# Splitting the output weights during the input projection and keeping both parts in DRAM

## The chip, the cores and the metric

The kernel runs on one core of a Trainium2 chip. The core has five instruction streams that matter here: TensorE (PE in the profile, with its weight loads shown apart as PEld), VectorE (DVE), ScalarE (ACT), GpSimd (POOL) and SyncE (SP), which in this kernel issues every data transfer (DMA). The metric is the device time of one execution in microseconds (us). The kernel before was timed in three runs: 2034.74, 2035.24 and 2037.11 us, median 2035.24 us. One further execution was taken under the hardware profiler; its own time was 2037.63 us and its span, from the first to the last instruction, 2035.9 us.

## The reference

One layer of a streaming encoder is computed for a prompt of 2048 frames and for 64 further frames ("sample") of a running stream with 4096 past frames. `D_MODEL` is 1024, and there are four heads of differential attention (branch A) and four of retention (branch B). Cut to what matters here:

```python
def layer_inputs(x, ...):
    h = rmsnorm(x, norm_g) @ w_in                     # 1024 -> 6144 columns
    qa, ka, va, za, qb, kb, vb, zb, ga, gb = jnp.split(h, ...)
    ...
    ga = jax.nn.sigmoid(ga + b_gate[0]); gb = jax.nn.sigmoid(gb + b_gate[1])

def layer_output(x, oa, ob, za, zb, ga, gb, ..., w_oa, w_ob, w_out):
    oa = (rmsnorm(oa, subln_g) * (1.0 - lam_init)).reshape(B, T, W_A) * jax.nn.silu(za)
    ob = rmsnorm(ob).reshape(B, T, W_B) * jax.nn.silu(zb)
    m = ga * (oa @ w_oa) + gb * (ob @ w_ob)           # w_oa, w_ob: 512 x 1024
    return x + m @ w_out                              # w_out: 1024 x 1024
```

Between the two stand the attention of branch A (prompt frames see their own and earlier chunks, the sample sees the past cache and itself) and the chunked recurrence of branch B. `w_oa` is the input `w_o_diff`, and `w_ob` is `w_o_ret`.

## The kernel before, in words

**Precision.** All large products run on operands in the fp32r format. To keep the accuracy, an operand x is split into a high part, `h` (x cast to fp32r on ScalarE), and a low part, `l` = x - h (a subtraction on GpSimd or VectorE). A product takes three matmuls: h·h, h·l and l·h. So each weight that TensorE uses has to be loaded, cast and subtracted first.

**Stages and streams.** Two streams run side by side. `w_stream` is the input projection: frames in two halves of 1024 (the first half carries the 64 sample frames too), and in each half 24 column tiles of 256 columns of `w_in`. `z_stream` is the attention and the retention: the four prompt heads of the first half, then in the first half the sample's attention (`sample_attn`), the sample's retention and retention blocks 0 to 7 (`ret_sample`, `ret_some`), then the same for the second half. When both are through, the output stage (`out_stream`) takes eight groups g of 256 frames (264 columns with the sample's): eight `m_tile`s per group (the products with `w_o_diff` and `w_o_ret`, 24 matmuls of 264 columns each), whose results `m_fin` multiplies by the gates and splits, and two `y_tile`s per group (the product with `w_out`, 48 matmuls of 512 columns each), plus one for the sample at the end.

**What sets the order.** The program is written out by a planner in Python (`loop`). Tasks are generators that yield the time or condition at which they can go on; the planner keeps a running estimate of each engine's time and always advances the ready task with the lowest priority number. `w_stream` has number 9 and `z_stream` 4, with helpers at 0 to 3, so that projection matmuls fill whatever TensorE time the other stream leaves. `out_stream` has 8. The orders on TensorE, ScalarE and VectorE are those in which the planner emits; SP and GpSimd are ordered by the tile framework. `take` and `give` count the buffers of a tag. `ld` and `st` put a DMA on SP.

**The weight pipeline of the projection.** `w_load` (lines 332 to 342) loads units of 256 rows by 256 columns (256 KB) into a staging tag `ws` of 3 buffers, in the order of `self.order`. `w_split` (line 344) takes two of the 12 buffers of tag `w`, one for the high and one for the low part, casts on ScalarE (line 354) and subtracts on GpSimd (line 361; twice, at the start, on VectorE), and appends the pair to the queue `wq`. A column tile (`natural` or `transposed`, whose matmuls are on line 384) takes four units and gives their `w` buffers back one by one during its last group of matmuls. 12 buffers are six units, so while a column tile is worked on, two units are split ahead, and three more are staged.

**The order of the first half.** `seq` in `w_stream` has, after the attention's columns, the tiles of vb, qb, kb (two each), a mark, za and zb (two each), ga and gb (four each).

**The output weights.** When `z_stream` is through, its buffers are closed, pool `z3` is opened and `load_wo` (line 1244) fetches `w_o_diff` and `w_o_ret`, in 32 pieces of 128 rows by 256 columns (128 KB). Each goes into one of the 9 buffers of tag `oz`, is cast on ScalarE (line 1232), and subtracted on GpSimd (line 1235, a third of them) or VectorE (line 1239). `out_prep` starts when the eighth pair of tiles is begun; its loads of attention output and z (three `oz` buffers per tile) feed `og_fin`, which makes the split operands of `m_tile`. When the projection is through, its pools are closed and pool `z4` is opened; there `gate_prep` loads the gates into the 6 buffers of tag `gt`, two for each `m_tile`, and `load_wout` fetches `w_out` in another 32 pieces, through the same `gt` buffers. `m_fin` gives two `gt` buffers back when it is through (line 1379). `m_tile` has two PSUM buffers for each branch, so that it runs at most two tiles ahead of `m_fin`.

Of the kernel before, what the change touches and what calls it, by code (L numbers as in the profile page):

```python
# [8 lines left out]
F32 = mybir.dt.float32  # L9
# [45 lines left out]
class Hybrid:  # L55
# [276 lines left out]
    def w_load(self):  # L332
        for half in range(2):
            for c0 in self.order[half]:
                for q in range(4):
                    yield from self.take("ws")
                    st = self.sb(self.wp, [128, 2, 256], "ws")
                    t = self.ld(st, self.i["w_in"][0, 256 * q:256 * q + 256, c0:c0 + 256]
                                .rearrange("(c p) n -> p c n", p=128), 1 << 18)
                    self.wst.append((st, t))  # L340
                    self.wloads += 1
                    yield self.pe

    def w_split(self):
        nc = self.nc
        for n in range(4 * (len(self.order[0]) + len(self.order[1]))):
# [873 lines left out]
    def split_load(self, stp, tag, h, l, src, n, slot):  # L1220
        for q in range(4):
            sl = slice(256 * q, 256 * q + 256)
            yield from self.take(tag)
            s = self.sb(stp, [128, GW], tag, "wst")[:, :256]
            t = self.ld(s, src[:, sl], 1 << 17)
            self.spawn(self.split_fin(tag, h[:, sl], l[:, sl], s, t, (n + q) % 3 == 0, slot), 2)
            yield self.pe

    def split_fin(self, tag, h, l, s, t, on_pool, slot):
        nc = self.nc  # L1230
        yield t
        nc.scalar.copy(h, s)
        t = self.A(256, self.pe)
        if on_pool:
            nc.gpsimd.tensor_sub(l, s, h.bitcast(F32))  # L1235
            t = self.G(256, t)
        else:
            yield t
            nc.vector.tensor_sub(l, s, h.bitcast(F32))
            t = self.V(256, t)  # L1240
        self.give(tag, t)
        slot.append(t)

    def load_wo(self):
        pool = self.z3
        for br, name in enumerate(("w_o_diff", "w_o_ret")):
            for kt in range(4):
                h = pool.tile([128, 1024], F32R, tag=f"{name}h{kt}", name=f"{name}h{kt}")
                l = pool.tile([128, 1024], F32R, tag=f"{name}l{kt}", name=f"{name}l{kt}")
                slot = []  # L1250
                self.wo[br].append((h, l, slot))
                yield from self.split_load(pool, "oz", h, l, self.i[name][0, 128 * kt:128 * kt + 128, :], kt, slot)

    def load_wout(self):
        pool = self.z4
        for ct in range(8):
            h = pool.tile([128, 1024], F32R, tag=f"woh{ct}", name=f"woh{ct}")
            l = pool.tile([128, 1024], F32R, tag=f"wol{ct}", name=f"wol{ct}")
            slot = []
            self.wout.append((h, l, slot))  # L1260
            yield from self.split_load(pool, "gt", h, l, self.i["w_out"][0, 128 * ct:128 * ct + 128, :], ct, slot)
# [62 lines left out]
    def m_tile(self, g, ct, og):  # L1324
# [3 lines left out]
        for br, tag in ((0, "mm"), (1, "s")):  # L1328
            yield from self.take(tag)
            ps = self.psum(tag)[:, :GW]  # L1330
            for kt in range(4):
                wh, wl, tw = self.wo[br][kt]
                if ct == 0:
                    yield lambda: len(self.ogs) > 8 * g + 4 * br + kt and self.ogs[8 * g + 4 * br + kt] and len(tw) == 4
                    og.append(self.ogs[8 * g + 4 * br + kt][0])
                    if max(*tw, og[-1][2]) > self.pe:
                        yield max(*tw, og[-1][2])
# [44 lines left out]
    def y_tile(self, g, sel, r, x, y):  # L1382
# [10 lines left out]
        for ct, nh in [(c, k) for k in range(2) for c in range(7)] + [(7, 0), (7, 1)]:  # L1393
            nsl, xt, tx, ps = run[nh]
            yield lambda: len(self.wout) > ct and len(self.wout[ct][2]) == 4 and len(self.mq[g]) > ct
# [6 lines left out]
            if max(t, *tw) > self.pe:  # L1402
                yield max(t, *tw)
# [38 lines left out]
    def w_stream(self):  # L1442
# [23 lines left out]
        seqs = [f + seq for f in first]  # L1466
        self.order = [[c for c, _ in q if c is not None] for q in seqs]
# [162 lines left out]
```

## Time and profile before

| quantity | value |
|---|---|
| median of three runs | 2035.24 us (2034.74 to 2037.11) |
| the profiled execution's own time | 2037.63 us |
| its span | 2035.9 us |
| PE busy | 1999.1 us, 98% |
| DVE busy | 985.9 us, 48% |
| ACT busy | 962.7 us, 47% |
| POOL busy | 420.5 us, 21% |
| moved by DMA | 281.57 MB, 138 GB/s in the mean |

The page gives each engine's busy time, then the span in 40 slices, the DMA queues, the chain of work that ended last, the costliest groups of instructions, and the DMA issues. Groups are rows of "line, engine, operation, output<-inputs, shapes, count | busy us, mean ns of one | idle time before them and what ended it". Durations of matmuls overlap, because they are pipelined: the time that one costs is the distance from its start to the next start. The view by windows gives busy time by engine in a stretch, with the granted clock of TensorE, the busy share of the 16 DMA engines and what they moved; for the instructions of one line it gives that line's share. Times in the timeline and in the chain are from the start of the span.

### The profile page before, as it was taken

Reading aid. Unit: us, or ns where it says so; the run is one execution under the profiler, and the core shown is the slowest. Engines: PE = TensorE matmul, PEld = TensorE weight load, DVE = VectorE, ACT = ScalarE, POOL = GpSimd, SP = SyncE. Lnnn points to the kernel's source line nnn. Section 1 sums busy time; section 2 is a strip of 40 time slices with the busy share of each in tenths; the row PEclk is TensorE's granted clock in tenths of the full one; section 3 lists DMA queues with packets and bytes.
Section 4 is the critical chain, followed back from the end, with each engine's and each line's share of the span. In section 5 each row is a group of like instructions: output and inputs, shape, how many; then the busy total and the mean of one; then the engine's idle time right before and its main releaser. Section 6 shows DMA issues by size and latency. Waiting matters only on the chain. (4 is left out here: it accounts for less than half of the span.)

```text
span 2035.9 us, 35819 instructions
## 1 busy us (share of the span) xinstructions
PE 1999.1 (98%) x13058; PEld 1826.1 (90%) x13058; DVE 985.9 (48%) x2671; ACT 962.7 (47%) x2123; POOL 420.5 (21%) x394
## 2 busy tenths in 40 slices
PE   7999999999999999999999999999999979999999
PEld 7999999999998999999999888888888868888997
DVE  6265765643331210546856545635653365444442
ACT  5334766644343332535766655634654453333321
POOL 1222112121012221221211212122131343222210
PEclk9999999999999999999999999999999989999999
DMA  6663545345565463563352252463233665454531
GB/s 217 202 195 115 162 138 145 101 124 156 151 170 133 130 194 93 152 200 127 113 155 91 84 154 75 115 188 99 63 100 113 187 200 154 144 150 136 148 101 58
DMA packets 332160, 281.57 MB, mean 138 GB/s; under 512 B 65104, under 2 KB 307408, under 8 KB 331984
## 3 DMA queue, kind: packets, MB, share of 16 engines
q1 hardware_dynamic: 331984, 279.29, 46.8%
q8 instruction: 103, 1.69, 0.4%
q14 instruction: 73, 0.60, 0.1%
HBM read 187.71 MB, written 91.49 MB: 137 GB/s over the span
## 5 line engine op out<-in xcount | busy, mean ns | idle before, releaser
L384 PE MATMUL mm<-xh,wh 128*128 128x512 f32 (+2 forms) x1280 | 459.8, 359 | 0.0
L384 PE MATMUL mm<-xh,wl 128*128 128x512 f32 (+2 forms) x1280 | 452.0, 353 | 0.0
L384 PE MATMUL mm<-xl,wh 128*128 128x512 f32 (+2 forms) x1280 | 451.7, 353 | 0.0
L361 POOL TENSOR_TENSOR wl<-ws,wh 128x512 fp32r<-128x512 f32 x190 | 252.1, 1342 | 832.5 <-ACT wh L354 643.5
L384 PE MATMUL mm<-wh,xh 128*128 128x256 f32 x1088 | 313.3, 288 | 0.5 <-ACT xh L315 0.3
L384 PE MATMUL mm<-wl,xh 128*128 128x256 f32 x1088 | 307.7, 283 | 0.7 <-DVE wl L358 0.3
L384 PE MATMUL mm<-wh,xl 128*128 128x256 f32 x1088 | 307.7, 283 | 0.2 <-DVE xl L316 0.2
L384 PEld LDWEIGHTS mm<-xh,wl 128*128 128x128 f32 x1280 | 241.0, 188 | 31.1
L384 PEld LDWEIGHTS mm<-xh,wh 128*128 128x128 f32 x1280 | 241.3, 189 | 30.6 <-issue 0.2
L384 PEld LDWEIGHTS mm<-xl,wh 128*128 128x128 f32 x1280 | 241.4, 189 | 30.0
L384 PEld LDWEIGHTS mm<-wh,xh 128*128 128x128 f32 x1088 | 204.8, 188 | 3.3 <-ACT xh L315 0.5
L384 PEld LDWEIGHTS mm<-wl,xh 128*128 128x128 f32 x1088 | 204.9, 188 | 3.0 <-DVE wl L358 0.5
L384 PEld LDWEIGHTS mm<-wh,xl 128*128 128x128 f32 x1088 | 204.7, 188 | 0.4 <-DVE xl L316 0.4
L569 ACT COPY ev<-mm 128x512 f32<-128x512 f32 x140 | 71.6, 512 | 213.4 <-PE mm L384 200.4
L865 DVE TENSOR_TENSOR atl<-at,ath 128x512 fp32r<-128x512 f32 (+1 forms) x144 | 93.6, 660 | 151.6 <-ACT ath L863 151.6
L782 ACT ACTIVATE row<-row,a_mx 128x1024 f32<-128x1024 f32 (+7 forms) x160 | 153.5, 963 | 24.2 <-DVE a_mx L762 24.0
L752 DVE CUSTOM_DVE_ANT_0 row<-s,dfar 128x512 f32<-128x512 f32 (+2 forms) x192 | 117.3, 631 | 72.4 <-PE s L744 71.3
L354 ACT CAST wh<-ws 128x512 fp32r<-128x512 f32 x192 | 117.0, 619 | 65.4 <-PE mm L384 37.5
L863 ACT CAST ath<-at 128x512 fp32r<-128x512 f32 (+1 forms) x144 | 79.6, 563 | 99.1 <-PE at L850 98.6
L743 PE MATMUL s<-K,q 128*128 128x512 f32 (+3 forms) x320 | 120.3, 381 | 3.0 <-DVE a_acc L752 2.8
L803 DVE SCALAR_TENSOR_TENSOR row<-row,a_w 128x1024 f32<-128x1024 f32 (+4 forms) x96 | 101.4, 1064 | 40.5 <-ACT row L800 40.2
L744 PE MATMUL s<-K,q 128*128 128x512 f32 (+3 forms) x320 | 115.7, 363 | 0.0
(196 smaller groups left out, 3922.1 us busy)
## 6 DMA issues: line engine op xcount, KB each, us to landing
ws<-in_w_in_dram SPq DMA_DIRECT2D x192, 256.0 KB, 3.0
q<-qT SPq DMA_DIRECT2D x128, 128.0 KB, 3.0
V<-vN SPq DMA_DIRECT2D x24, 512.0 KB, 5.4
K<-kT SPq DMA_DIRECT2D x48, 256.0 KB, 4.2
gt<-gaT SPq DMA_DIRECT2D x64, 132.0 KB, 2.1
gt<-gbT SPq DMA_DIRECT2D x64, 132.0 KB, 2.1
xt<-in_x_prompt_dram SPq DMA_DIRECT2D x16, 512.0 KB, 5.0
kn<-in_cache_k_T_dram SPq DMA_DIRECT2D x32, 256.0 KB, 3.2
```

The source lines that it names most:

```text
L354: nc.scalar.copy(h, st)
L361: nc.gpsimd.tensor_sub(l, st, h.bitcast(F32))
L384: nc.tensor.matmul(ps, p, q, start=c == 0 and i == 0, stop=c == KC - 1 and i == 2)
L569: nc.scalar.copy(ev, ps)
L743: nc.tensor.matmul(ps, q1s, kk, start=True, stop=False)
L744: nc.tensor.matmul(ps, q2s, kk, start=False, stop=True)
L752: nc.vector.tensor_tensor_reduce(out=units[k0 // 1024][:, k0 % 1024:k0 % 1024 + n], in0=ps, in1=tab, scale=-SLOPES[h], scalar=3.0e38, op0= ...
L782: nc.scalar.activation(u, u, AF.Exp, bias=mx, scale=-1.0, accum_out=lp[:, k:k + 1])
L803: nc.vector.scalar_tensor_tensor(out=u0, in0=u0, scalar=w[:, 0:1], in1=u1, op0=ALU.mult, op1=ALU.add)
L863: nc.scalar.copy(ah[:, :w], at[:, :w])
L865: nc.vector.tensor_sub(al[:, :w], at[:, :w], ah[:, :w].bitcast(F32))
```

## The change

Scratch tensors `wsp` are added in DRAM: a high and a low part for each of `w_o_diff`, `w_o_ret` (512 x 1024) and `w_out` (1024 x 1024), 16 MB together. In the first half's sequence, after each of the first six tiles of the row za0, za1, zb0, zb1, ga0, ga1, two new items stand. The eight items of the two smaller weights hold two units each (a column block of 256 over 512 rows), the four items of `w_out` hold four. So four units follow za0, za1, zb0 and zb1 each, and eight units follow ga0 and ga1 each: 32 units. They go through `w_load` and `w_split` in their place in the order; then, instead of matmuls, `presplit` takes them from `wq` and stores both parts to DRAM, and the two `w` buffers come free when the second store has landed.

In the output stage the 64 pieces with their casts and subtractions (`split_load`, `split_fin`) are gone. `load_pair` loads 128 rows by 1024 columns of each part (512 KB) straight into the tile that TensorE reads: 16 loads for the two smaller weights and 16 for `w_out`. After issuing a pair it waits until the planner's estimate for that DMA has passed. `oz` and `gt` buffers are no longer taken for weights.

```diff
+        self.wsp = {n: [tc.dram_tile([k, 1024], F32, name=f"{n}{j}") for j in range(2)]
+                    for n, k in (("w_o_diff", 512), ("w_o_ret", 512), ("w_out", 1024))}
...
     def w_load(self):
+        for name, c0, nq in self.order:
+            for q in range(nq):
+                yield from self.take("ws")
+                st = self.sb(self.wp, [128, 2, 256], "ws")
+                t = self.ld(st, self.i[name][0, 256 * q:256 * q + 256, c0:c0 + 256]
+                            .rearrange("(c p) n -> p c n", p=128), 1 << 18)
...
-    def split_load(self, stp, tag, h, l, src, n, slot):
-    def split_fin(self, tag, h, l, s, t, on_pool, slot):
+    def presplit(self, name, c0, nq):
+        for q in range(nq):
+            yield lambda: len(self.wq) > 0
+            h, l, t = self.wq.pop(0)
+            if t > self.pe:
+                yield t
+            for j, w in enumerate((h, l)):
+                ts = self.st(self.wsp[name][j][256 * q:256 * q + 256, c0:c0 + 256]
+                             .rearrange("(c p) n -> p c n", p=128), w.bitcast(F32), 1 << 18)
+            self.give("w", ts, 2)
             yield self.pe
...
+    def load_pair(self, pool, name, kt, tag, out):
+        rows = slice(128 * kt, 128 * kt + 128)
+        w = []
+        for j in range(2):
+            u = pool.tile([128, 1024], F32R, tag=f"{tag}{j}{kt}", name=f"{tag}{j}{kt}")
+            t = self.ld(u.bitcast(F32), self.wsp[name][j][rows, :], 1 << 19)
+            w.append(u)
+        out.append((w[0], w[1], t))
+        yield t - DMA_LAT
...
     def load_wo(self):
+                yield from self.load_pair(self.z3, name, kt, name, self.wo[br])
     def load_wout(self):
+            yield from self.load_pair(self.z4, "w_out", ct, "wo", self.wout)
...
+        out = [("w_o_diff", c, 2) for c in range(0, 1024, 256)] + \
+              [("w_o_ret", c, 2) for c in range(0, 1024, 256)] + [("w_out", c, 4) for c in range(0, 1024, 256)]
+        late = len(seq) - 12
+        mid = seq[:late]
+        for k, item in enumerate(seq[late:]):
+            mid.append(item)
+            if k < 6:
+                mid += [(o, None) for o in out[2 * k:2 * k + 2]]
+        seqs = [first[0] + mid, first[1] + seq]
...
+                elif f is None:
+                    yield from self.presplit(*c0)
```

In `m_tile` and `y_tile` the waits for four pieces per weight tile become one wait for the pair's load.

More of the change, by code (lines that the diff above doesn't have):

```diff
@@ L332, in w_load @@
     def w_load(self):
[L333 to L342, printed above, removed]
+        for name, c0, nq in self.order:
[4 more added lines that the diff above has]
+                            .rearrange("(c p) n -> p c n", p=128), 1 << 18)
+                self.wst.append((st, t))
+                self.wloads += 1
+                yield self.pe
     def w_split(self):
         nc = self.nc
-        for n in range(4 * (len(self.order[0]) + len(self.order[1]))):
+        for n in range(sum(o[2] for o in self.order)):
             yield lambda: len(self.wst) > 0
@@ L1218, in ret_sample @@
         self.state, self.t_state = None, 0.0
-    def split_load(self, stp, tag, h, l, src, n, slot):
[L1221 to L1226, printed above, removed]
-            yield self.pe
-    def split_fin(self, tag, h, l, s, t, on_pool, slot):
[L1230 to L1242, printed above, removed]
+    def presplit(self, name, c0, nq):
[8 more added lines that the diff above has]
+            self.give("w", ts, 2)
+            yield self.pe
@@ L1256, in load_wout @@
         for ct in range(8):
[L1257 to L1261, printed above, removed]
+            yield from self.load_pair(self.z4, "w_out", ct, "wo", self.wout)
     def out_prep(self):
@@ L1333, in m_tile @@
                 if ct == 0:
-                    yield lambda: len(self.ogs) > 8 * g + 4 * br + kt and self.ogs[8 * g + 4 * br + kt] and len(tw) == 4
+                    yield lambda: len(self.ogs) > 8 * g + 4 * br + kt and self.ogs[8 * g + 4 * br + kt]
                     og.append(self.ogs[8 * g + 4 * br + kt][0])
-                    if max(*tw, og[-1][2]) > self.pe:
-                        yield max(*tw, og[-1][2])
+                    if max(tw, og[-1][2]) > self.pe:
+                        yield max(tw, og[-1][2])
                 oh, ol, _ = og[4 * br + kt]
@@ L1394, in y_tile @@
             nsl, xt, tx, ps = run[nh]
-            yield lambda: len(self.wout) > ct and len(self.wout[ct][2]) == 4 and len(self.mq[g]) > ct
+            yield lambda: len(self.wout) > ct and len(self.mq[g]) > ct
             h, l, t = self.mq[g][ct]
@@ L1465, in w_stream @@
                             self.transposed(half, dst, 2 * g, final=fin)))
-        seqs = [f + seq for f in first]
-        self.order = [[c for c, _ in q if c is not None] for q in seqs]
+        out = [("w_o_diff", c, 2) for c in range(0, 1024, 256)] + \
[7 more added lines that the diff above has]
+        seqs = [first[0] + mid, first[1] + seq]
+        self.order = [c if isinstance(c, tuple) else ("w_in", c, 4) for q in seqs for c, _ in q if c is not None]
         self.seg_free = [0.0, 0.0]
```

11 lines of the change are left out of this document (2 added, 9 removed).

## The prediction

> **What bounds the kernel now.** I read the page first: which engine is busy, and where in the 40 slices it is not.
>
> ```profile
> span 2035.9 us, 35819 instructions
> PE 1999.1 (98%) x13058; PEld 1826.1 (90%) x13058; DVE 985.9 (48%) x2671; ACT 962.7 (47%) x2123; POOL 420.5 (21%) x394
> PE   7999999999999999999999999999999979999999
> ```
>
> TensorE is busy all the time, except in the first slice and in slice 33, where the output stage begins. So a change that leaves the matmuls as they are can gain only what that slice lacks, and any stretch in which it makes TensorE wait is lost in full. Then the waits of TensorE, the timeline around slice 33 and the chain that ended last:
>
> ```profile
> PE mm L1339 <- DVE gt L1359: 7.4, 4, 2.9
> PE s L1339 <- ACT ogh L1298: 4.6, 2, 4.3
> PE at L1404 <- ACT mh L1369: 2.0, 1, 2.0
> ```
> ```profile
> 1634.12 0.40 PE L384 MATMUL mm<-xh,wl 128*128 128x512 f32 x1
> 1634.36 0.28 PE L1339 MATMUL mm<-ogh,w_o_diffh 128*128 128x264 f32 x1
> 1634.48 0.28 PE L1340 MATMUL mm<-ogl,w_o_diffh 128*128 128x264 f32 x1
> 1642.71 0.59 PE L1339 MATMUL s<-ogh,w_o_reth 128*128 128x264 f32 x1 [4.30 <-ACT ogh L1298]
> 1643.78 0.42 PE L1339 MATMUL mm<-ogh,w_o_diffh 128*128 128x264 f32 x1
> 1644.00 0.42 PE L1340 MATMUL mm<-ogl,w_o_diffh 128*128 128x264 f32 x1
> ```
> ```profile
> 1688.95 0.70 DVE oyt L1418
> 1734.56 0.70 DVE oyt L1418
> ```
>
> The projection's last matmul starts at 1634.12, the first `m_tile` at 1634.36, and the first finished output tile is added at 1688.95: 54.6 us. Starts are 0.12 us apart for 264 columns when the clock is full (1634.36, 1634.48). One whole group takes 1734.56 - 1688.95 = 45.6 us, with 192 matmuls of 264 columns and 96 of 512; 192 x 0.122 = 23.4, so one of 512 takes (45.6 - 23.4) / 96 = 0.23 us. Up to the first finished output tile there are 192 of the one kind and 45 of the other, 33.8 us. So the beginning of the output stage costs 20.8 us too much: about 6.5 before 1643.78 (the second `m_tile`), 14.3 behind it. That is the whole of what can be won.
>
> **What goes in the output stage.** Splitting goes, 64 pieces; the groups of `w_out`, with two of the queue's rows, show the main part:
>
> ```profile
> L1232 ACT CAST woh<-wst 128x256 fp32r<-128x256 f32 x32 | 12.2, 402 | 3.8 <-DMA wst<-in_w_out_dram 3.5
> L1239 DVE TENSOR_TENSOR wol<-wst,woh 128x256 fp32r<-128x256 f32 x21 | 12.2, 613 | 1.6 <-ACT woh L1232 1.1 <-DMA wst<-in_w_out_dram 0.4
> L1235 POOL TENSOR_TENSOR wol<-wst,woh 128x256 fp32r<-128x256 f32 x11 | 9.9, 903 | 14.9 <-ACT woh L1232 14.9
> 1610.07 0.92 SPq L130 DMA_DIRECT2D wst<-in_w_o_ret_dram  x2
> 1637.70 0.37 SPq L130 DMA_DIRECT2D gt<-gaT  x1
> 1638.12 1.63 SPq L130 DMA_DIRECT2D gt<-gbT  x1
> gt<-gbT SPq DMA_DIRECT2D x64, 132.0 KB, 2.1
> L1320 ACT ACTIVATE gt<-gt,bg 128x264 f32<-128x264 f32 x128 | 59.0, 506 | 7.9 <-DMA gt<-gaT 6.6 <-DMA gt<-gbT 1.3
> ```
>
> ACT, DVE and POOL are relieved of 12.2, 12.2 and 9.9 us just there, and the gates get all six `gt` buffers; four `PE mm <- DVE gt` waits (7.4 us, above) come from gates that arrived late. The casts and subtractions of the two smaller weights ran under the projection's matmuls and cost nothing; that cover stays.
>
> What stays late: the gates cannot be loaded before 1637.70, when the projection's buffers are free, and `out_prep` still waits for the eighth pair. Now 16 loads of 512 KB come instead of 32 of 128 KB. The nearest rate for 4 KB rows is the kernel's beginning, for rows of 1 KB the two lower rows:
>
> ```profile
> 10.00:15.00 5.00, 3.37 (x22) 2.72 (x23) 3.78 (x8) 3.21 (x8) 0.94 (x2) 1.00 1.03 403
> 690.00:695.00 5.00, 5.00 (x29) 4.31 (x28) 0.61 (x1) 1.07 (x2) 2.12 (x2) 1.00 1.07 238
> 1595.00:1600.00 5.00, 5.00 (x24) 4.14 (x23) 2.20 (x4) 2.58 (x6) 1.61 (x3) 1.00 0.94 293
> ```
>
> 8.4 MB at 403 GB/s are 20.8 us: the first 16 loads end about when the old ones were issued (1610.07), so the first `m_tile` gains nothing; the second 16 run from 1637.7 to about 1659, before `y_tile` needs them, but gate loads queue among them. Of 14.3 us I take 4.3 as left for that. Gain 10 us; between 18 and a loss of 2. The 18 leave 2.8 us: two `m_tile`s without gates end at 1634.4 + 5.8 = 1640.2, and the first gate pair is on ScalarE's far side at 1638.1 + 1.6 + 2.1 + 0.5 = 1642.3, with the multiplication behind it near 1643. The loss stands for gates held up behind all 16 loads.
>
> **What comes in the first half.** The splits themselves are 32 x (0.62 + 1.34) us on ACT and POOL, which are half and a fifth busy: nothing. The buffers are the cost. Rows of the pipeline, and the projection's share of TensorE by line 384 alone:
>
> ```profile
> L361 POOL TENSOR_TENSOR wl<-ws,wh 128x512 fp32r<-128x512 f32 x190 | 252.1, 1342 | 832.5 <-ACT wh L354 643.5 <-PE mm L384 97.5 <-PE at L850 55.4
> L354 ACT CAST wh<-ws 128x512 fp32r<-128x512 f32 x192 | 117.0, 619 | 65.4 <-PE mm L384 37.5 <-DMA ws<-in_w_in_dram 20.4 <-issue 4.1
> ws<-in_w_in_dram SPq DMA_DIRECT2D x192, 256.0 KB, 3.0
> gaT<-ev SPq DMA_DIRECT2D x24, 256.0 KB, 2.6
> ```
> ```profile
> 510.00:550.00 40.00, 25.26 (x140) 21.76 (x141) 1.00 0.57 154
> 592.00:611.00 19.00, 8.30 (x40) 6.60 (x40) 1.00 0.48 134
> 660.00:690.00 30.00, 19.47 (x112) 16.77 (x112) 1.00 0.43 122
> ```
>
> Before, a column tile used four units and left two split ahead and three staged, and its successor started at once. Now, at its end (T), two of the output weights' units are ready and nothing of the next column tile. The next tile's fourth unit is behind everything that `presplit` has to move, since a staging buffer comes free only as units are split, and a `w` buffer only as stores land. At 293 GB/s, 256 KB take 0.9 us.
>
> After ga0 and ga1 (eight units): 16 stores and 7 loads lie between T and that unit, 23 x 0.9 = 20.6 us; then the rest of the last landing (3.0 - 0.9), cast 0.62, subtraction 1.34, and six matmuls 1.4: its first group ends at T + 26. Unhindered, the group's 24 matmuls are 5.5 us at the projection's 65% share (19.47 of 30): T + 8.5. So the projection stands still for 17.5 us. The attention has priority already and does not lack TensorE, so what the projection gives up is idle: 17.5 x 0.65 = 11.4 us, twice, 23. Bounds: 10 if the pipeline moves at 403 GB/s and retention takes 56% of TensorE as in 592 to 611 (23 x 0.65 + 5.5 - 8.5 = 12, x 0.44, twice), 35 if nothing fills (17.5 twice).
>
> After za0, za1, zb0 and zb1 (four units): 8 stores and 3 loads, 9.9 + 5.5 = T + 15, against T + 8.7: 6.5 us. The other stream here is the sample's attention, and its next cast waits mostly for TensorE itself, that is, for projection matmuls ahead of it:
>
> ```profile
> L945 ACT CAST ath<-kn 128x512 fp32r<-128x512 f32 x32 | 19.2, 622 | 11.8 <-PE s L912 10.4 <-PE pv L1027 1.4
> ```
>
> So it speeds up when the projection stops. I take 3 us each, 12 together; bounds 2 (filled almost whole) and 17 (6.5 x 0.65, four times).
>
> SP issues all of it: 64 stores and 32 loads more in this stretch, 96 x 0.4 us over some 200 us. A store that waits for its split holds up the attention's loads behind it; its K and V have four buffers ahead, so I put this at nothing, and in the bounds above.
>
> **The clock.** After the wait of 4.30 us, starts are 0.22 apart instead of 0.12 (1643.78, 1644.00), at a granted clock of 0.61 to 0.70:
>
> ```profile
> 1640.00:1645.00 5.00, 2.29 (x9) 2.11 (x10) 1.88 (x5) 3.29 (x9) 1.25 (x2) 0.61 0.73 222
> 1645.00:1650.00 5.00, 5.00 (x32) 5.00 (x31) 4.33 (x9) 2.39 (x7) 3.30 (x5) 0.70 0.84 246
> ```
>
> 0.39 of the 2.29 busy us and 0.30 of 5.00 are 2.4 us lost. I take one such event at each of the two long stops, 5 us; bounds 0 and 14 (six). The Trainium skill (TensorE: Matmul & The Clock Gate, the table of clock states) says that the array falls to half rate after an idle window of about 3.4 us. By that rule the long stops fall under it, the short ones only where the attention does not break them up, and the sum would be the same or up to 10 us higher; this trace agrees with it at 4.30 us of idle.
>
> One rule would take something off. The Trainium skill (DMA: Bandwidth & Descriptors, Measured) gives 341 GB/s for transfers of 1 MB. As an estimate from that page, 23 transfers would take 17.7 us instead of 20.6, and the two long stops 3.8 us less together; the trace's 293 at a DMA share of 0.94 and 238 at 1.07, for rows of 1 KB, speak against it here.
>
> **The sum.** -10 + 23 + 12 + 5 = +30 us on the profiled execution's 2037.6 (span 2035.9), so 2067.6; that execution is 2.4 above the median of the runs, so I forecast **2065 us**, slower.
>
> **Rivals.**
> - *The stops are filled* (ends faster). Place: the six column tiles behind the new items. If the other stream could use TensorE nearly whole whenever the projection stops, nothing idles, and the gain of 10 to 18 is left: at least 2 + 2 for small gaps, so 2021 to 2031. It decides where less than 10 us idle at the six places together. For it: the cast that waits for TensorE (10.4 of 11.8 us), and 56% in 592 to 611. Against it: retention is a chain of short steps, and the bursts of stores delay its loads.
> - *Nothing is won at the output and the stops are whole*: the gates queue behind 8.4 MB (+2), 35 + 17 in the stops, up to 8 for the clock: up to 2097; about 2090. For it: the share of 0.65, which is what the projection has when the attention is already served first.
> - *The stops are halved*: stores land faster than loads of the same size (2.6 against 3.0 us above), buffers come back earlier: 10 + 4 in the stops, 2 for the clock, -10: about 2041.
> - *The change doesn't do what it says*: the loads are no more ready than before, since `z4` opens no earlier. With 8.4 MB instead of 4.2 behind 1637.7, `y_tile` would wait for its eighth pair. At 403 GB/s it lands at 1659, at 238 at 1673, and `m_tile`s at full speed from 1643.8 end at 1664: up to 9 us given back, inside the bounds of the output term.
>
> **How the numbers follow.** A measurement of this kernel can tell about 0.2%, 4 us, from no change. Chances: my forecast (2048 to 2084) 0.62; stops filled 0.16; halved 0.11; nothing won 0.11. Faster by over 0.2%, below 2031: 0.17, nearly all of it the first rival. Within: 0.05, the edge between the first and third. Slower: 0.78. The range goes from 2028 to 2088: it leaves out most of the first rival and the upper half of the second. The likeliest case's own range is 2048 to 2084.
>
> **What would show it.** Right: TensorE idle, waiting for GpSimd's `wl` on line 384 or for loads into `ws`, in six places between about 465 and 720 us, two of them long; a granted clock below 1 there; slices of 8 or less in the page's PE row between 10 and 15; DMA share near 1 there; line 1235's and 1239's groups gone; the way from the first `m_tile` to the first finished output tile about 44 us instead of 54.6. Wrong: PE at 9 throughout the first half (then the stops are filled), or the output stage still at 54 us. The prediction fails most easily in how much of TensorE attention and retention take when the projection stands still; the trace of before has no stretch of them alone.

## The result and the profile after

The changed kernel takes 2093.64 us (median of four runs, 2092.82 to 2094.2) where the kernel before takes 2034.99: 1.0285 times as long, interval 1.027 to 1.0301. It is slower, as forecast, but by 58.6 us and not by 30, and 5.6 us above the range. The profiled execution took 2093.39 us, its span is 2091.6 us. From the page of the changed kernel, busy time of TensorE, its 40 slices and the granted clock:

```profile
span 2091.6 us, 35757 instructions
PE 2015.8 (96%) x13058; PEld 1837.7 (88%) x13058; DVE 969.0 (46%) x2630; ACT 955.0 (46%) x2091; POOL 440.5 (21%) x403
PE   8999999999998799999999999999999969999999
PEclk9999999999998999999999999999999979999999
```

The number of matmuls is the same, and TensorE has gaps in two slices (627 to 732 us) that it didn't have. The view by windows from 400 to 800 us, first the kernel before in one row, then the changed kernel (us, then busy time and count of PE, PEld, DVE, ACT, POOL, then granted clock, DMA share, GB/s):

```profile
400.00:800.00 400.00, 398.54 (x2631) 366.63 (x2630) 114.45 (x328) 152.02 (x354) 71.95 (x58) 1.00 0.52 142
```
```profile
400.00:500.00 100.00, 94.41 (x593) 85.75 (x592) 43.14 (x121) 43.49 (x97) 18.87 (x16) 0.98 0.55 166
500.00:600.00 100.00, 91.18 (x584) 83.49 (x583) 32.58 (x101) 45.41 (x108) 20.87 (x17) 0.97 0.70 207
600.00:700.00 100.00, 87.27 (x564) 78.16 (x565) 24.11 (x59) 34.98 (x87) 29.83 (x25) 0.88 0.73 211
700.00:800.00 100.00, 88.03 (x558) 81.23 (x557) 23.64 (x48) 31.26 (x73) 30.90 (x24) 0.95 0.62 189
```

TensorE idles 39.1 us of these 400 (before: 1.5), and the granted clock falls below one, which it did not before. Summed over the eighty 5-us windows, busy time times what the clock lacks to one, that is another 12.7 us. The gaps stand where the prediction put them. The main waits of TensorE in the changed kernel, and the first rows behind three of the gaps:

```profile
PE pv L1028 <- ACT atp L1056: 15.1, 4, 4.4
PE tp L1178 <- DVE rru L1172: 14.0, 3, 7.1
PE mm L1328 <- ACT ogh L1287: 8.9, 3, 6.4
PE s L1328 <- ACT ogh L1287: 6.5, 3, 3.0
```
```profile
463.47 0.58 PE L1028 MATMUL pv<-vc,atp 128*128 128x128 f32 x1 [4.42 <-ACT atp L1056]
705.56 0.66 PE L1178 MATMUL tp<-ident,rru 128*128 128x128 f32 x2 [3.47 <-DVE rru L1172]
719.71 1.09 PE L1178 MATMUL tp<-ident,rru 128*128 128x128 f32 x4 [7.07 <-DVE rru L1172]
```

Four short stops of 4.42, 1.92, 4.40 and 4.40 us lie at 459, 506, 549 and 598 us; the two long ones are broken up by small pieces of work into 3.43, 2.0, 1.5 and 2.6 us (647 to 661) and 3.47 and 7.07 us (702 to 720). The first work to come behind a stop is mostly the other stream's: the projection itself stands still for longer. None of its matmuls starts between 457.79 and 474.83 us at the first place, nor between 701.78 and 726.30 at the last; the longest such gap in the kernel before (from 440 to 740 us) is 10.2 us. So the profile puts only 4.1 us down to the weights themselves (`wh`, `wl`), where the prediction had looked for the waits.

The projection's last matmul starts at 1687.93 instead of 1634.12: 53.8 us. From there to the first finished output tile it takes 56.95 us (1744.88) where it took 54.83. So the output stage gained nothing and lost 2 us. Its waits changed kind, though: those of `m_tile` for the gates (7.4 us before) are gone, and those for `ogh` rose from 4.6 to 15.4 us. The issue queue of SP shows why:

```profile
1673.11 0.47 SPq L130 DMA_DIRECT2D z<-zaT  x1
1678.13 11.24 SPq L130 DMA_DIRECT2D gbT<-ev  x3
1689.46 0.42 SPq L130 DMA_DIRECT2D z<-zaT  x1
1691.55 0.32 SPq L130 DMA_DIRECT2D gt<-gaT  x1
```

The first load for `og_fin` is issued 15 us ahead of the projection's end; before, it was 23 us (1611.08 against 1634.12). `out_prep` still waits until the eighth pair is begun, and a pair is now begun only when the planner's time for the pair before it has passed. The fourth z load then stands behind three stores of the projection's last tiles, which hold SP for 11.24 us. TensorE waits for `ogh` until 1711.5 and is granted half the clock.

### The profile page after: what moved, and what is told of

Read it like the earlier page. It is cut to its first block, busy times and chain, and to the rows that moved or that the text cites. A ratio compares the mean times of both kernels' runs of the same rounds, so it can differ in the third digit from the quotient of the medians.

```text
span 2091.6 us, 35757 instructions
## 1 busy us (share of the span) xinstructions
PE 2015.8 (96%) x13058; PEld 1837.7 (88%) x13058; DVE 969.0 (46%) x2630; ACT 955.0 (46%) x2091; POOL 440.5 (21%) x403
## 4 chain that ended last, share of the span: by engine, by line
PE 89%; DVE 3%; ACT 3%; DMA 2%; issue 2%; SPq 1%; POOL 0%; POOLq 0%; ACTq 0%; DVEq 0%
PE mm L385 49%; PE s L744 3%; PE s L745 3%; PE at L1393 3%; PE at L1395 3%; PE at L1394 3%; PE at L851 3%; PE pv L831 2%; PE pv L830 2%; PE pv L829 2%; PE s L1328 1%; PE s L1329 1%; PE mm L1328 1%; PE s L1330 1%; PE mm L1330 1%
## 5 line engine op out<-in xcount | busy, mean ns | idle before, releaser
L362 POOL TENSOR_TENSOR wl<-ws,wh 128x512 fp32r<-128x512 f32 x222 | 291.0, 1325 | 888.4 <-ACT wh L355 678.9
L355 ACT CAST wh<-ws 128x512 fp32r<-128x512 f32 x224 | 135.7, 620 | 59.3 <-PE mm L385 33.2
```

The costliest lines, as they stand in the source:

```text
L355: nc.scalar.copy(h, st)
L362: nc.gpsimd.tensor_sub(l, st, h.bitcast(F32))
```

## Experiments

All ratios are to the kernel before, timed on the same chip.

**The two halves apart.** `e1_output_alone` keeps the new loads of the output stage and drops the items in the line; the loads read scratch of the same size that exists anyway:

```diff
-            t = self.ld(u.bitcast(F32), self.wsp[name][j][rows, :], 1 << 19)
+            t = self.ld(u.bitcast(F32), self.kT[j][kt % 4, :, 1024 * (kt // 4):1024 * (kt // 4) + 1024], 1 << 19)
...
-            if k < 6:
-                mid += [(o, None) for o in out[2 * k:2 * k + 2]]
```

> The changed kernel without the twelve items in the first half: 16 + 16 loads of 512 KB in the output stage, but nothing stored before. Left out: the split of the output weights; both parts are read from the scratch of the keys (same size, same rows of 4 KB), so the outputs are not the reference's. Theory A (the output part by itself wins nothing, because out_prep starts its loads only behind the eighth pair; the trace of the changed kernel has 57 us from the first m_tile to the first finished output tile against 54.6): 2034 to 2040 us. Rival B (the output part wins about 10 us as forecast, and the first half costs more than it shows): 2022 to 2028.

`e2_first_half_alone` is the reverse: the kernel before with `wsp`, the items, `w_load`, `w_split` and `presplit` of the changed kernel, its output stage untouched.

> The kernel before, with the twelve items of the first half (loads, splits and stores to the scratch), but the output stage as before: it splits its weights itself and does not read the scratch. Theory A (39 us idle and 13 us of lowered clock between 400 and 800 us are the whole loss): 2085 to 2090 us. Rival B (the first half costs more, the output part gives 10 back): 2097 to 2105.

Measured: e1 2036.73 us, 1.0006 (0.9996 to 1.0015); e2 2093.12 us, 1.0281 (1.0261 to 1.0302). e1 is as theory A has it, e2 lies between its two expectations. The first half is the whole loss, 57 us, and the output part is worth nothing by itself.

**Where the output's gain went.** `e3_output_early` is e1 without one wait; `e8_before_early` takes that wait from the kernel before for group 0 alone:

```diff
     def out_prep(self):
-        yield lambda: len(self.wo[1]) == 4
```

> As the output part alone, but out_prep does not wait for the eighth pair of weight tiles: its first loads go ahead of the weights. Left out: as there. Theory A1 (the late start of out_prep is what takes the gain): the way from the first m_tile to the first finished output tile falls from about 57 to 40-45 us, 2020 to 2026 us in all. Rival A2 (the gates are held up behind the 8.4 MB of w_out, whenever out_prep starts): still 50 us or more, 2032 to 2040.

> The kernel before, where only the first group's loads of out_prep do not wait for the eighth pair; weights are split in the output stage as before. Theory G (the late start alone took the gain, the splits in the way hardly matter): 2022 to 2028 us. Rival H (the splits of w_out hold the gates, as the four waits on the gates' product say: 7.4 us and the clock stay): 2030 to 2036 us.

Measured: e3 2023.66 us, 0.9936 (0.9919 to 0.9953); e8 2033.69 us, 0.9991 (0.9981 to 1.0). The rows by windows at the beginning of the output stage, e1 first, then e3:

```profile
1640.00:1650.00 10.00, 2.89 (x9) 2.17 (x9) 3.61 (x7) 3.56 (x9) 2.30 (x4) 0.50 1.02 362
```
```profile
1640.00:1650.00 10.00, 7.29 (x56) 6.71 (x55) 4.50 (x13) 3.93 (x9) 2.61 (x4) 1.00 0.99 372
```

The DMA engines are just as full in both (362 and 372 GB/s), but in e3 the operands of the first `m_tile`s were fetched before, and from the projection's last matmul to the first finished output tile (1675.02) it takes 41 us. Ready loads alone give 0, the early start alone 2 us at most (its interval touches 1), both together 12. The two have to come together, since either leaves the other's wait standing: between 1600 and 1720 us, e1 still waits 15.1 us for `ogh`, and e8 10.2 us for the gates.

**Are the stores to blame?** The prediction's stops were made of transfers, two thirds of them stores. `e4_no_stores` leaves the stores out and the rest in; `e17_no_staging` leaves out the loads and the staging buffers too (in both, the output stage reads the same other scratch as in e1):

```diff
-            for j, w in enumerate((h, l)):
-                ts = self.st(self.wsp[name][j][256 * q:256 * q + 256, c0:c0 + 256]
-                             .rearrange("(c p) n -> p c n", p=128), w.bitcast(F32), 1 << 18)
-            self.give("w", ts, 2)
+            self.give("w", self.pe, 2)
```
```diff
+                if name != "w_in":
+                    self.wst.append((None, 0.0))
+                    continue
...
+            if out:
+                st = self.ident.unsqueeze(1).to_broadcast([128, 4, 128])
```

> The changed kernel with all 32 units loaded and split in their place in the first half, but not stored: presplit gives the buffers back at once. Left out: the stores; the output stage reads the keys' scratch in their place, so the outputs are not the reference's. Theory S (the stores' bytes make the stops: without them 7 units lie before the next column tile's fourth, 7 x 0.9 + 4.1 + 1.4 = 12 us against 8.5 unhindered at the two long stops, nothing at the four short ones): 5 to 12 us above the output part alone, 2040 to 2050 us. Rival L (the units' place in the line makes them, whatever is done with them: 3 staging buffers, one turn of each 3.0 + 0.62 + 1.34 us): 2070 to 2090 us.

> e4_no_stores with one change: the 32 units of the output weights are not loaded either and take none of the three staging buffers; their rounding and subtraction are done on a constant that lies in SBUF, in the same places of the line (the outputs are wrong, as the scratch is never written). Theory G (what delays is the turn of the three staging buffers, about 6 us for three units, through which the projection's own weights must pass behind the output's): 2084.8 falls to 2040 to 2060 us, idle of TensorE between 400 and 800 us from 30 to under 15 us. Rival E (what delays is that the conversions stand ahead of the projection's in the order of ScalarE and GpSimd and in the six pairs): 2072 to 2086 us, idle over 22 us.

Measured: e4 2084.83 us, 1.0241 (1.022 to 1.0261); e17 2079.9 us, 1.022 (1.0203 to 1.0237). Both are in the range of the rival in their expectation (L, E). From 400 to 800 us, e4, then e17:

```profile
400.00:800.00 400.00, 369.72 (x2353) 338.27 (x2352) 118.65 (x328) 158.51 (x367) 102.91 (x83) 0.95 0.53 152
```
```profile
400.00:800.00 400.00, 372.91 (x2384) 342.24 (x2383) 117.27 (x328) 158.81 (x369) 104.30 (x85) 0.95 0.47 134
```

Without a single byte of the output weights moved in the first half, 27.1 of 39.1 us idle remain, and 44 of the 57 us. The stores take about 9 us (1.0285 to 1.0241). Staging and loads take about 4 by the medians, but the intervals of e4 and e17 overlap. Neither the stores nor the staging buffers are the main cause. By place there is one exception, the last of the two long stops; the changed kernel, e4 and e17:

```profile
690.00:740.00 50.00, 38.03 (x269) 35.85 (x268) 24.89 (x52) 21.18 (x55) 20.17 (x16) 0.90 0.75 226
```
```profile
690.00:740.00 50.00, 44.03 (x303) 40.61 (x302) 19.69 (x47) 22.00 (x57) 21.15 (x16) 0.97 0.62 170
```
```profile
690.00:740.00 50.00, 47.60 (x342) 45.01 (x341) 16.95 (x51) 23.39 (x59) 20.10 (x17) 0.97 0.47 137
```

Here idle falls from 12.0 to 6.0 and 2.4 us as stores, then loads and staging go. At the other long stop (640 to 690 us) it is 10.4, 10.9 and 9.2 us, and before 640, with the four short ones, 16.7, 13.4 and 15.5.

**Is it the place in the line?** `e6_spread` has the same 32 units, stores included, but two behind each of the last 16 column tiles of the first half instead of four or eight behind six:

```diff
+            if item[0] is not None and len(mid) > 1 and out:
+                mid.append((out.pop(0), None))
```

> The changed kernel with the same 32 units, loads, splits and stores, but two units behind each of 16 column tiles of the first half in place of four or eight behind each of six. Theory L (the stop is the time in which the pipeline of 3 staged and 2 split-ahead units fills again; two units more than the lookahead empties, and the next tile's four are ready or staged): no stops of more than a microsecond or two, 2037 to 2050 us. Rival S2 (each unit in the line costs its 1.5 us wherever it stands, about 48 us over 32 units): 2080 to 2095 us.

Measured: 2072.39 us, 1.018 (1.0165 to 1.0195), between the two expectations; idle falls to 14.7 us. Four stops of 2.55 us are left, at 460, 506, 554 and 602 us (and one of 2.61 at 722), and the first is not DMA (share 0.02 in 460 to 465). The rows of ScalarE just there, first in the kernel before, then in e6:

```profile
453.29 0.62 ACT L354 CAST wh<-ws 128x512 fp32r<-128x512 f32 x1 [0.36 <-PE mm L384]
454.50 0.62 ACT L354 CAST wh<-ws 128x512 fp32r<-128x512 f32 x1 [0.59 <-PE mm L384]
455.38 0.62 ACT L354 CAST wh<-ws 128x512 fp32r<-128x512 f32 x1 [0.26 <-PE mm L384]
...
457.08 0.71 ACT L972 ACTIVATE row<-row,s_mx 128x512 f32<-128x512 f32 x1
```
```profile
456.24 0.71 ACT L973 ACTIVATE row<-row,s_mx 128x512 f32<-128x512 f32 x1
...
461.18 0.71 ACT L973 ACTIVATE row<-row,s_mx 128x512 f32<-128x512 f32 x1
...
461.89 1.64 ACT L355 CAST wh<-ws 128x512 fp32r<-128x512 f32 x3
```

Eight exponentials of the sample's softmax hold ScalarE for 6 us. Before, three casts of the next tile's weights ran ahead of them; in e6 they come behind, and TensorE stands from 459.99 to 462.54. `e12_softmax_open` tests whether that block is the cause, with `e13_before_open` as its control:

```diff
             for m in range(8):
+                yield self.act
                 u = units[m // 2][:, (m % 2) * 512:(m % 2) * 512 + 512]
```

> e6_spread with one change: the eight exponentials of a sample head are no longer put on ScalarE's queue as one block of 6 us, the roundings of weights that are ready may come between them. Theory Q (the roundings stand behind the block on ScalarE's in-order queue, and TensorE has used up its weights by then): the four stops of 2.55 us at 460, 506, 554 and 602 us are gone, idle between 400 and 800 us falls from 14.7 to 3 to 8 us, and the time from 2072.4 to 2052 to 2064 us. Rival W (the weights' buffers or loads were late anyway, the block only happens to be there): the stops stay within 1 us of 2.55, 2068 to 2077 us.

> The kernel before with the same one change as e12_softmax_open: the control. It has no stop at these four places, so theories Q and W both expect no change worth the name, 2032 to 2039 us; a gain of more than 4 us here would mean that what e12_softmax_open gains has nothing to do with the output weights.

Measured: e12 2070.13 us, 1.0173 (1.0158 to 1.0188); e13 2036.26 us, 1.0002 (0.9993 to 1.0012). The waits of e12:

```profile
PE mm L385 <- ACT wh L355: 5.3, 2, 4.4
PE pv L1029 <- ACT atp L1057: 6.7, 4, 2.2
PE pv L1029 <- DMA vc<-in_cache_v_diff_dram: 4.8, 3, 2.5
```

The casts did slip in between (456.71, 457.94), and the four waits for `wh` are gone, as theory Q had it (the two that the first row still has lie outside 400 to 800 us). The time is rival W's: idle is 15.5 us where it was 14.7. The waits only changed their names. The block decides what TensorE waits for; that it has nothing else to do comes from something else.

`e18_ahead_kept` moves the two output units of a tile from in front of the next tile's four units to the middle of them, and gives their buffers back in a task of their own; `e9_spread_early` and `e19_ahead_early` are e6 and e18 with the early `out_prep`:

```diff
+                self.order += [("w_in", c0, 0), ("w_in", c0, 1)]
+                if k == 0 and i >= len(cols) - 16:
+                    self.order += [out.pop(0), out.pop(0)]
+                self.order += [("w_in", c0, 2), ("w_in", c0, 3)]
...
+            if name == "w_in":
+                self.wq.append((h, l, t))
+            else:
+                self.spawn(self.presplit(name, c0, q, h, l, t), 0, "w")
```

> e6_spread with the two output units of a column tile moved from in front of the next column's four units to the middle of them, and given back by a task of their own as soon as their stores have landed: at the end of a column tile the two pairs that lie ahead hold weights of the next column tile, as in the kernel before, and not output weights. Theory H (what costs is that the output's units take these two pairs, so that TensorE starts the next column tile with nothing ahead): e6_spread's 2072.4 falls to 2040 to 2055 us, idle between 400 and 800 us from 14.7 to under 6 us. Rival E (the conversions' work and order on ScalarE and GpSimd at the column's end cost, wherever the pairs are): 2062 to 2076 us, idle over 10 us.

> As the spread order, and out_prep does not wait for the eighth pair. If the two effects add: 13 us below the spread order. If the first half's stops move the end of the other stream so that nothing is early: no gain over the spread order.

> e18_ahead_kept with the output's gates let start without waiting for the eighth pair: 12 to 16 us less than e18_ahead_kept by all theories, as from e6_spread to e9_spread_early; with theory H 2026 to 2041 us.

Measured: e18 2058.7 us, 1.0113 (1.0096 to 1.013), idle 9.3 us between 400 and 800; e9 2057.23 us, 1.0104 (1.0088 to 1.0119); e19 2044.76 us, 1.0045 (1.003 to 1.006). Keeping the next tile's weights ahead wins 13.7 us, less than theory H asked for and more than rival E: the time falls between their ranges (2040 to 2055 and 2062 to 2076), and so does the idle time. e18 also takes the storing out of the projection's own task, and the two effects are not told apart. The early start gives 15 and 14 us in these two; e19 misses theory H's range for it (2026 to 2041) by 4 us. In e18 the casts still come behind the exponentials, and one stop of 4.42 us at 820 us, in the second half, is there that the kernel before does not have. Of e18's remaining cost over e1, 22 us, 19.5 are seen: idle of 9.3 and 8.8 us in 400 to 800 and 800 to 1100 against 0 and 3.8, and 5.2 us of clock. That the exponentials' place against the tile's end sets the stops that are left is argued, not shown. The stop at 820 us looks alike: the cast that ends it (823.59) stands on ScalarE behind five squares of the second half's input tiles (L279, from 816.12 on). e6 and e12 have it too, with 4.42 us at 834 and 828.

**The same work out of the line.** `e7_apart_early` splits 128-row pieces in `z_stream`, behind the retention of the first half, in `row` buffers. `e10_idle_buffers` does it behind the sample's attention in the `K` and `V` tiles, idle until the second half's heads, and `e14_idle_vector` is e10 with the subtraction on VectorE. All three have the early `out_prep`. The diff from e7 to e10:

```diff
-                yield from self.take("row", 3)
-                s = self.row("ps")
+                yield from self.take("K", 2)
+                yield from self.take("V")
+                s = self.sb(self.ap, [128, 1024], "K", "ps")
...
                 yield from self.sample_attn()
+                self.spawn(self.presplit(), 4, "z")
...
-        nc.vector.tensor_sub(l, s, h.bitcast(F32))
+        nc.gpsimd.tensor_sub(l, s, h.bitcast(F32))
```

> Nothing in the projection's line: the output weights are split in the other stream, between the first half's retention and the second half's attention, in its own idle row buffers (16 loads of 512 KB, 16 casts, 16 subtractions on VectorE, 32 stores of 512 KB), and out_prep does not wait. Theory L (only the place in the line costs; traffic and engine time are free): 2020 to 2027 us, as the output part with the early start alone. Rival T (loads, splits and stores cost by themselves): 2033 us or more.

> The output weights are split as a task of the attention stream, out of the line of the projection's weights, in the K and V tiles that nobody uses between the last sample head and the second half's heads; the gates start early as in e3_output_early and e7_apart_early. Theory P (what costs is the place in the line and the sharing of buffers that others wait for: w and ws in the changed kernel, row in e7_apart_early): the time is that of e3_output_early, 2021 to 2029 us, idle of TensorE between 400 and 1100 us under 6 us, the second half's input tiles loaded from about 740 us on. Rival T (the work itself costs, 24 MB of traffic and 32 more instructions on ScalarE and GpSimd): 2034 to 2050 us, near e7_apart_early's 2045.6, with idle of 10 us or more spread over the stretch in which the splits run.

> e10_idle_buffers with one change: the subtraction of the split is on VectorE (0.69 us at 512 columns, so about 1.4 us each) instead of GpSimd (2.39 us each in e10_idle_buffers). Theory X (VectorE's short instructions stand still while a GpSimd subtraction runs: rows of 128x4 that take 161 ns in the kernel before took 754 to 988 ns in e10_idle_buffers, and TensorE waited for the retention's end behind them): these rows are back under 250 ns, the stops of 2.01, 1.77 and 1.62 us at 702, 750 and 769 us are gone, 2021 to 2027 us. Rival Y (what holds the retention is ScalarE's 1.07 us roundings ahead of it, or the traffic): the stops stay, 2028 to 2033 us.

Measured: e7 2045.61 us, 1.0045 (1.0028 to 1.0061), in rival T's range; e10 2030.72 us, 0.9978 (0.9969 to 0.9987); e14 2028.71 us, 0.9968 (0.9956 to 0.998). In e7 the first half has no idle (0.7 us), but the second half's input tiles share the `row` buffers and are loaded late; the first such load in the kernel before, then in e7:

```profile
739.86 0.37 SPq L130 DMA_DIRECT2D xt<-in_x_prompt_dram  x1
```
```profile
807.40 0.52 SPq L130 DMA_DIRECT2D xt<-in_x_prompt_dram  x1
```

There TensorE idles 18.0 us between 800 and 1100. In buffers that nobody waits for, splitting the same weights costs 6.5 us over e3 (e14, 0.9968 against 0.9936; for e10, which falls between theories P and T, 8.5), where in the line it costs 34 over e3 spread out (e9) and 57 as the change has it. So e14 is a version of the change that is faster than the kernel before, by 0.32%.

Of the 7.0 us by which e10's span is longer than e3's, 5.4 lie in stops of 2.01, 1.77 and 1.62 us behind the retention. The groups of VectorE between 600 and 800 us, first in e10, then in e14:

```profile
L229 DVE TENSOR_TENSOR sm_t<-sm_t,ms 128x4 f32<-128x4 f32 (+1 forms) x9 | 8.9, 988 | 0.3
L230 DVE SCALAR_TENSOR_TENSOR sm_y<-sm_t,sm_y 128x4 f32<-128x4 f32 (+1 forms) x9 | 6.8, 754 | 0.3
```
```profile
L230 DVE SCALAR_TENSOR_TENSOR sm_y<-sm_t,sm_y 128x4 f32<-128x4 f32 (+1 forms) x9 | 2.5, 281 | 0.3
L229 DVE TENSOR_TENSOR sm_t<-sm_t,ms 128x4 f32<-128x4 f32 (+1 forms) x9 | 2.5, 278 | 0.3
```

In the kernel before these rows show 161 and 162 ns, in the changed kernel 626 and 389. They stretch while a GpSimd subtraction runs; with fewer of those, they shrink (not quite under the 250 ns of theory X) and the three stops are gone. In place of them stands one of 3.14 us at 650, for `wl`: on GpSimd, three subtractions of the projection's weights stand behind one of retention's instructions that waits for a load. So the stops went as theory X has it, and the time stayed in rival Y's range; the intervals of e10 and e14 overlap, and a gain is not shown. `e15_after_vector` puts every subtraction of the changed kernel on VectorE, `e16_before_vector` those of the kernel before:

```diff
-            if n in (0, 2):
+            if True:
```

> The changed kernel with every weight's subtraction on VectorE, none on GpSimd. Theory X: the stop of 3.47 us at 702 us goes (VectorE's four instructions ahead of it took 5.14 us there against 1.17 us in the kernel before, 3.97 more) and that of 7.07 us at 713 us shrinks by about 3 us; with the clock that comes to 7 to 14 us, so 2079 to 2087 us. Rival Z (those stops come from weights that are late, the VectorE rows only happen to end last): 2088 to 2096 us, with the stops at 702 and 713 us as long as before.

> The kernel before with the same change as e15_after_vector, the control: 2032 to 2039 us by both theories. A gain of more than 4 us would mean that e15_after_vector's has nothing to do with the output weights.

Measured: e15 2095.09 us, 1.0291 (1.0275 to 1.0306); e16 2042.76 us, 1.0039 (1.0024 to 1.0054). The waits of e15:

```profile
PE s L1101 <- DMA rqk<-kbT: 10.5, 2, 5.9
PE tp L1178 <- DVE rru L1172: 7.1, 3, 3.6
```

Waits behind `rru` halved (14.0 to 7.1 us), as theory X had it, and those for loads of `rqk` rose from 2.6 to 10.5. No time is won. The control is worse by 7 us, and 5 of them are a lower granted clock in the first 50 us (7.3 us lost instead of 2.2); e15 loses the same there (7.2), so it may hide a gain of that size. The stretched rows are real, but no cause of the loss that these runs can show.

## Why the prediction was right or wrong

- *Slower, by stops of TensorE in six places, two of them long, with a lower clock*: right. Of the 55.7 us between the two spans, 53.8 lie before the projection's end.
- *The stops, 35 us idle (23 and 12)*: 37.6 us more idle than before; the long ones sum to 9.5 and 10.5 us where 11.4 each was forecast, the short ones to 15.1 instead of 12. The size was right.
- *The cause of the stops*: wrong in the main, and it is the step "23 x 0.9 = 20.6 us", by which transfers set the length of the stops. Taking out all 16 stores would leave by that working 7 x 0.9 + 5.5 = T + 11.8 against T + 8.5, about 2 us per long stop and none at the short ones. Measured without stores: 30.3 us idle of 39.1; only the last long stop shrank with the transfers (12.0 to 6.0 and 2.4 us). That the sum fitted was luck and did not bear out its terms. What the runs show in its place is the units' stand in the projection's line: e6 wins 21 us by having fewer units in one place, e18, which against e6 changes only where they stand and how their buffers come back, another 13.7, and outside the line all but 6.5 us of the 57 go. That fits the sentence before the step in the prediction, that nothing of the next tile is ready at a tile's end; 22 us of e18's loss remain, so it is not the whole of it.
- *The casts and subtractions "nothing"*: wrong as part of the line. In e17 they and the `w` buffers that they take are all that is left there, and 44 us stay. Busy shares say how much an engine does, not what stands in front of what in its order. Out of the line, in e14, they are near nothing.
- *The clock, 5 us*: 12.7 measured, within the bounds of 0 to 14. I counted two events, and three of the four short stops lower the clock as well (0.69 in 550 to 555); the one of 1.92 us does not (1.00 in 505 to 515).
- *The output stage, -10 us*: wrong, 0 by itself (e1) and +2 in the changed kernel, at the edge of its bounds. The step is "the first `m_tile` gains nothing": it loses, because the later start of `out_prep` puts its z loads behind stores on SP. From the first `m_tile` (1689.97) to the first finished output tile it takes 54.9 us, not 44, which the prediction itself had named as a sign of being wrong. The gate waits went as forecast, and 12 us were there to be won (e3), but behind that condition.
- *Sum*: 37.6 + 12.7 + 2.1 = 52.4 of 55.7 us; where the rest lies stays open. Against the forecast's 30, the output term is off by 12.1 us, the clock by 7.7 and the stops by 2.6. So the output term put the time outside the range: had it been -10, the time would have been about 2082. The rival "nothing is won at the output and the stops are whole", about 2090 us, came nearest, and only in part by its own terms: its output term of +2 was measured, its 52 us of stops were 37.6. It deserved more than its chance of 0.11, since the prediction itself says that `out_prep` still waits for the eighth pair.

## What to carry to other kernels

Work that is put into another loop's software pipeline can cost far more than its bytes or its engine time (here 57 us, 9 of them for the stores, where the same work outside the line cost 6.5); ask what it displaces there, the items that should have been ready at the next tile's start, look for a task with buffers of its own that are idle at that time, and see who next takes those buffers. Before a wait is removed, list the other conditions of the same start, since two waits that end together give nothing one at a time. And a forecast whose sum comes out right can have the wrong cause: take out the term that is blamed, and see whether its microseconds go.

## What the hardware showed unexpectedly

**Short stops can lower the clock too.** Windows behind some of the stops, in e6 (two behind 2.55 us, one behind 2.61) and then in e12 (behind 1.48, 2.17 and 2.47 us):

```profile
465.00:470.00 5.00, 5.00 (x35) 4.82 (x34) 0.61 (x1) 1.10 (x2) 2.26 (x3) 0.76 0.78 201
510.00:515.00 5.00, 4.86 (x19) 4.33 (x19) 0.00 (x0) 0.75 (x3) 2.69 (x3) 0.50 0.54 142
725.00:730.00 5.00, 4.97 (x39) 4.80 (x40) 1.93 (x5) 0.90 (x3) 3.62 (x3) 1.00 0.73 180
```
```profile
465.00:470.00 5.00, 3.96 (x35) 3.96 (x36) 1.78 (x5) 2.61 (x5) 3.64 (x3) 1.00 0.36 110
510.00:515.00 5.00, 4.26 (x24) 4.26 (x25) 0.86 (x3) 2.31 (x5) 3.73 (x3) 0.67 0.41 120
605.00:610.00 5.00, 2.53 (x19) 2.19 (x18) 0.69 (x1) 0.59 (x1) 0.00 (x0) 1.00 1.04 308
```

Idle is nearly the same in both kernels (14.7 and 15.5 us between 400 and 800), but e6 loses 10.1 us to the clock there and e12 2.8. So four stops of 2.55 us cost nearly as much again behind them, and the fifth, of 2.61 us at 722, nothing; of e12's, the one of 2.17 us gives 0.67 in a window, those of 1.48 and 2.47 none. A stop of 1.92 us lowers the clock in e4 (0.78 in 555 to 560) and not in the changed kernel (1.00 in 505 to 510). The length alone does not decide at these lengths; what else does stays open. The Trainium skill (TensorE: Matmul & The Clock Gate, the table of clock states) puts the fall at an idle window of about 3.4 us; some of these stops are shorter and the clock falls all the same, so here the measurement decides.

**VectorE is held up by GpSimd.** The Trainium skill (GPSIMD Engine Reference, Specifications) says that GpSimd's interfaces to SBUF are shared with VectorE, with contention for instructions that read two tensors from SBUF. The rows above agree: instructions of 128x4 with two SBUF inputs (`sm_t<-sm_t,ms`) went from 161 to 988 ns on average, six times as long. A latency chain of such tiny instructions can so be stretched by bulk work on another engine that looks free.
